# Attention in a hybrid encoder block: score products handed out one bank at a time, the meta keys' transposes moved to the end of their unit, and two reads of PSUM banks put first

## The chip, the cores and the metric

The program runs on one core of a Trainium2 chip. The metric is device microseconds of one execution. The kernel before took 1441.15 us, the median of three runs (1440.94 to 1446.21). A separate profiled execution took 1447.76 us, and its trace is the source of every duration below. Of the engines, TensorE is PE in the profile (its weight loads are PEld), VectorE is DVE, ScalarE is ACT, GpSimd is POOL, and SyncE, which only issues DMAs, is SP.

## The reference, cut to what matters

The block puts 16 meta tokens ahead of 1024 positions of width 1024 (1040 rows in all) and runs a mixer (attention with a forgetting term beside a diagonal state space model with a gated linear unit), an output projection and a gated convolutional feed-forward network. The part that most of the change touches is the attention:

```python
log_f = log_sigmoid(f_logit + b_forget)
cum_f = cumsum(log_f, axis=1)
# per block of 128 queries, 8 heads of width 64:
s = einsum('bqhd,bkhd->bhqk', qb, k) * scale + cum_f[query] - cum_f[key]
s = where(key_position <= query_position, s, -1e30)
p = softmax(s, axis=-1)
out = einsum('bhqk,bkhd->bqhd', p, v)
```

## The kernel before

All matmuls take 32-bit operands that are split into a high and a low part, so that a dense product is three matmuls (`dense_steps`, L172 to L174: high by high, low by high, high by low). TensorE's results go to PSUM banks in four tags: `mm` (three banks, dense products), `sp` (two, scores), `tp` (two, transposes) and `po` (one, the sum over keys). A bank is written again only when whoever reads it has done so.

**Order.** The program is written as one stream per operation, and a scheduling layer orders each engine's instructions. In the attention the order on TensorE is fixed by hand: `pin` (L807) ties each matmul to the one before. `after(a, b)` (L132) only orders two instructions of one program; it moves an instruction behind another one in its queue. Every engine runs its queue in order, so an instruction that waits holds all that stand behind it.

**Attention.** The eight heads come in four pairs. A pair has eight units: four groups of query tiles, here called A (tiles 0, 1, 2; tile 0 is the meta tokens), B (3, 4), C (5, 6) and D (7, 8), each for both heads (`shapes`, `units`). A unit of tiles c and c+1 goes through `pv` (L854):

- `scores` (L813) makes the softmax weights of one tile. Per bank of up to 512 keys it issues two products (L838, L839) into an `sp` bank; VectorE reads the bank with a fused add and running minimum (L844, twice where the diagonal block is in it) into `pt`; ScalarE then takes the exponential (L849), VectorE the reciprocal (L850), and GpSimd scales `pt` (L851). A tile has 1, 2 or 3 banks (tile 8 has three: 352, 352 and 336 keys). `pt` has four buffers, taken in turn (tiles 0 and 1 share one).
- `meta_keys` (L865) transposes the columns of the 16 meta keys of every tile of the unit (L870) into a `tp` bank; ScalarE (L872) and VectorE (L137, `tm`) copy them as high and low part.
- `turn` (L875) transposes one group of two key blocks (L885, up to four transposes) into a `tp` bank, copied out as `th` (L888) and `tl` (L137).
- The products with the values (L911) add four matmuls per group into `po`, and one last product with the meta keys (L914) ends the unit. `po` is then read by L916 and L917.

`fill(part)` (L933) places dense matmuls of the next pair's projection and of the gates between these steps, as many as `UW` gives the unit. The order in a unit before is: `meta_keys`, `turn` of the first group, `fill`, all score products of the next unit's last tile (`ahead`), then per group: `turn` of the next group, `fill`, the products; with the last group, all score products of the first tile (or two) of the unit after next (`behind`). Units A have one group, B two, C three, D four.

**Earlier, around 180 to 200 us.** `forget` (L532) computes the forgetting logits into three `mm` banks; ScalarE (L545) and VectorE (L546) read each, the middle one in two parts (columns 248 and 136). In the same queues stand the casts and splits of the linear unit's operands (`load_z`, L636: casts L648 and L670, low parts L137, one difference on GpSimd at L664). The next dense products on TensorE, the query projection, take the same banks in turn.

**Behind the attention.** When the last L914 has run, the memory of the attention is free, and SP loads `mr`, `ga` and `wr` (L1053, L1052, L1074) there. TensorE works on one gate chunk meanwhile (72 matmuls that are ordered behind the last L911), then on the attention's output product (L1118 to L1120); VectorE reads its banks (L1121), and `out_forms` (L1080) casts (L1097) and splits (L137, `xhi<-wr`) the output weights.

Of the kernel before, what the change touches and what calls it, by code (L numbers as in the profile page):

```python
# [25 lines left out]
H = 8  # L26
# [32 lines left out]
def block_kernel(ctx, tc, x, meta, xbt, x0t, g1t, w_q, w_k, w_v, w_f, w_u, w_g, b_f, w_ao, lam_d, bw_d, cw_d,  # L59
# [347 lines left out]
    for k0, n in FIRST:  # L407
        j, sl = k0 // 2, slice(k0 % 2, k0 % 2 + n)
# [121 lines left out]
    FR = 32 + H  # L530

    def forget():  # L532
# [3 lines left out]
        for t, n in BLK:  # L536
            ps = mm_ps()
            for i in range(KD):
                PE.matmul(ps[:64, :n], wf[:, i, :], xhi[:, i, t:t + n], start=(i == 0), stop=False)
                PE.matmul(ps[:64, :n], wf[:, i, :], xlo[:, i, t:t + n], start=False, stop=(i == KD - 1))  # L540
            for r, a in ((0, 0), (32, HL)):
                lo, up_ = max(t, a), min(t + n, a + HL)
                if lo < up_:
                    sl, ri = slice(lo - a, up_ - a), slice(r, r + H)
                    S.copy(fx[ri, sl], ps[32 - r:32 - r + H, lo - t:up_ - t])  # L545
                    V.scalar_tensor_tensor(out=fl_[ri, sl], in0=ps[ri, lo - t:up_ - t], scalar=bf[ri], in1=fx[ri, sl],  # L546
                                           op0=ALU.add, op1=ALU.add)
# [88 lines left out]
    def load_z():  # L636
# [23 lines left out]
        for k in range(2):  # L660
# [6 lines left out]
            for f_, t_ in zip((fa, fa, fb, fb), (T1, T2, T3, T4)):  # L667
                q = 0 if t_ is T1 or t_ is T3 else TH
                hi, lo = t_[0][:, k], t_[1][:, k]
                after(S.copy(hi, f_[:, q:q + TH]), ssm_outs[6])  # L670
# [142 lines left out]
    def scores(t_, e, c, fb):  # L813
# [21 lines left out]
        for b in range(nb):  # L835
            a0, a1 = b * w, min(kc, b * w + w)
# [15 lines left out]
        return pt  # L852

    def pv(h, cs, pts, ob, ahead, behind):  # L854
# [37 lines left out]
        part = 1 / (1 + len(groups))  # L892
        meta_keys()
        nxt = turn(groups[0])
        if len(groups) > 1:
            fill(part)
            ahead()
        else:
            ahead()
            fill(part)  # L900
        for g_, grp in enumerate(groups):
            th, tl = nxt
            if g_ + 1 < len(groups):
                nxt = turn(groups[g_ + 1])
            else:
                behind()
            fill(part)
# [12 lines left out]
    UW = {2: 1.2, 4: 1.0, 6: 0.95, 8: 0.9}  # L920
# [60 lines left out]

    def scores_of(u, which):
# [9 lines left out]
        pts_of.setdefault(u, [])  # L992
        for c in (cs[:-1] if which == 0 else cs[-1:]):
            pts_of[u].append(scores(tiles_of[pr], e, c, fbs[pr, e]))
# [4 lines left out]
    for u, which, n in ((0, 0, 7), (0, 1, 14), (1, 0, 7)):  # L999
        scores_of(u, which)  # L1000
        take(n)
        cnt -= n
    for u, (pr, cs, e) in enumerate(units):
# [10 lines left out]
        pv(2 * pr + e, cs, pts_of.pop(u), obs[cs], lambda: scores_of(u + 1, 1), lambda: scores_of(u + 2, 0))  # L1014
# [65 lines left out]
    def out_forms(p, j):  # L1080
# [17 lines left out]
        if p in (0, 4):  # L1098
            split_lo(V, slot[3], b_, slot[2])
# [979 lines left out]
```

## Time and profile before

| what | us |
|---|---|
| median of three runs | 1441.15 |
| profiled execution, its own time | 1447.76 |
| span of its trace | 1444.9 |
| TensorE busy | 1416.6 (98%) |
| VectorE busy | 1071.6 (74%) |
| ScalarE busy | 719.8 (50%) |
| GpSimd busy | 760.5 (53%) |

The page counts an engine as busy while an instruction of it runs. Matmuls overlap: the next one starts before the one ahead has ended, so the distance from one start to the next is what a matmul costs TensorE, and the duration in a row is longer than that. An idle time in a row stands in brackets, with whoever ended it. The trace's clock begins at the first instruction.

### The profile page before, as it was taken

Reading aid. Unit: us, or ns where it says so; the run is one execution under the profiler, and the core shown is the slowest. Engines: PE = TensorE matmul, PEld = TensorE weight load, DVE = VectorE, ACT = ScalarE, POOL = GpSimd, SP = SyncE. Lnnn points to the kernel's source line nnn. Section 1 sums busy time; section 2 is a strip of 40 time slices with the busy share of each in tenths; the row PEclk is TensorE's granted clock in tenths of the full one; section 3 lists DMA queues with packets and bytes.
Section 4 is the critical chain, followed back from the end, with each engine's and each line's share of the span. In section 5 each row is a group of like instructions: output and inputs, shape, how many; then the busy total and the mean of one; then the engine's idle time right before and its main releaser. Section 6 shows DMA issues by size and latency. Waiting matters only on the chain.

```text
span 1444.9 us, 26277 instructions
## 1 busy us (share of the span) xinstructions
PE 1416.6 (98%) x9607; PEld 1337.8 (93%) x9607; DVE 1071.6 (74%) x2050; ACT 719.8 (50%) x1405; POOL 760.5 (53%) x866
## 2 busy tenths in 40 slices
PE   8999999999999999999999999999999999999997
PEld 8999989988999999899879999999999999888886
DVE  7999778843667675647469987788777875798867
ACT  7646575423556565532645544444443445553443
POOL 1542248642455555515871244555645446699695
PEclk9999999999999999999999999999999999999999
DMA  8685634530144432157964155677654227863443
GB/s 297 174 183 164 153 96 125 169 118 30 38 154 111 140 81 68 45 190 245 279 151 144 61 150 146 163 183 204 173 142 106 88 93 248 323 224 124 131 95 117
DMA packets 92533, 214.02 MB, mean 148 GB/s; under 512 B 14658, under 2 KB 22466, under 8 KB 92020
## 3 DMA queue, kind: packets, MB, share of 16 engines
q1 hardware_dynamic: 73700, 168.15, 35.0%
q0 software_dynamic: 17696, 41.29, 15.0%
q10 hardware_dynamic: 1008, 2.91, 0.6%
q8 instruction: 75, 1.23, 0.3%
q14 instruction: 54, 0.44, 0.1%
HBM read 170.88 MB, written 71.71 MB: 168 GB/s over the span
## 4 chain that ended last, share of the span: by engine, by line
PE 90%; DMA 3%; POOL 2%; DVE 2%; ACT 1%; issue 1%; SPq 0%; POOLq 0%; DVEq 0%; ACTq 0%
PE mm L173 5%; PE mm L172 5%; PE mm L174 5%; PE sp L235 4%; PE sp L234 4%; PE sp L236 4%; PE mm L236 3%; PE mm L234 3%; PE tp L235 3%; PE tp L234 3%; PE mm L235 3%; PE tp L236 3%; PE po L911 2%; PE mm L1602 2%; PE mm L1600 2%; PE mm L1601 2%
## 5 line engine op out<-in xcount | busy, mean ns | idle before, releaser
L172 PE MATMUL mm<-xhi,whi 128*128 128x342 f32 (+2 forms) x480 | 158.0, 329 | 2.6 <-DVE fg L546 2.6
L173 PE MATMUL mm<-xlo,whi 128*128 128x342 f32 (+2 forms) x480 | 156.7, 326 | 0.0
L174 PE MATMUL mm<-xhi,wlo 128*128 128x342 f32 (+2 forms) x480 | 155.4, 324 | 0.0
L1222 POOL TENSOR_TENSOR ov<-ov,og 128x1024 f32<-128x1024 f32 x21 | 50.8, 2421 | 116.8 <-ACT og L1221 114.4
L137 DVE TENSOR_TENSOR sw<-sf,sw 128x512 fp32r<-128x512 f32 x72 | 71.7, 996 | 46.7 <-ACT sw L1213 46.7
L1213 ACT CAST sw<-sf 128x512 fp32r<-128x512 f32 x72 | 44.9, 624 | 110.2 <-POOL sf L1360 75.7
L172 PEld LDWEIGHTS mm<-xhi,whi 128*128 128x128 f32 x480 | 91.1, 190 | 3.5 <-issue 3.4
L174 PEld LDWEIGHTS mm<-xhi,wlo 128*128 128x128 f32 x480 | 90.9, 189 | 0.3 <-issue 0.2
L173 PEld LDWEIGHTS mm<-xlo,whi 128*128 128x128 f32 x480 | 91.1, 190 | 0.1
L849 ACT ACTIVATE pt<-pt,mx 128x400 f32<-128x400 f32 (+5 forms) x72 | 53.1, 737 | 61.7 <-DVE mx L844 61.0
L1360 POOL TENSOR_TENSOR sf<-raw 128x512 f32<-128x512 f32 x36 | 49.9, 1386 | 64.4 <-DMA raw<-in_w_up_dram 28.8
L1360 POOL TENSOR_TENSOR sf<-raw,sf 128x512 f32<-128x512 f32 x36 | 61.1, 1697 | 38.9 <-DVE sw L137 38.8
L236 PE MATMUL mm<-xhi,sw 128*128 128x258 f32 (+1 forms) x288 | 81.1, 282 | 0.0
L234 PE MATMUL mm<-xhi,sw 128*128 128x258 f32 (+1 forms) x288 | 80.9, 281 | 0.0
L235 PE MATMUL mm<-xlo,sw 128*128 128x258 f32 (+1 forms) x288 | 80.8, 281 | 0.0
L1412 DVE SCALAR_TENSOR_TENSOR ov<-hv,cwt,ov 128x1024 f32<-128x1024 f32 x36 | 70.8, 1967 | 0.4 <-ACT ov L1410 0.4
L851 POOL TENSOR_SCALAR pt<-pt,mx 128x400 f32<-128x400 f32 (+5 forms) x72 | 50.6, 704 | 32.2 <-DVE mx L850 26.6
L1213 ACT CAST sw<-raw 128x512 fp32r<-128x512 f32 x70 | 43.0, 620 | 47.3 <-PE sp L236 24.9
L137 DVE TENSOR_TENSOR tl<-tp,th 128x512 fp32r<-128x512 f32 (+1 forms) x80 | 50.9, 636 | 13.3 <-ACT th L888 12.5
L137 DVE TENSOR_TENSOR sw<-raw,sw 128x512 fp32r<-128x512 f32 x70 | 56.2, 806 | 4.7 <-ACT sw L1213 4.4
L822 POOL CAST qz<-q 64x128 fp32r<-64x128 f32 (+1 forms) x72 | 20.0, 281 | 75.2 <-PE sp L839 74.0
L888 ACT CAST th<-tp 128x512 fp32r<-128x512 f32 (+1 forms) x80 | 43.0, 537 | 29.8 <-PE tp L885 28.3
(724 smaller groups left out, 5732.1 us busy)
## 6 DMA issues: line engine op xcount, KB each, us to landing
raw<-in_w_up_dram SPq DMA_DIRECT2D x44, 512.0 KB, 3.8
t_d<-in_w_dn_dram POOLq DMA_DIRECT2D x44, 256.0 KB, 6.9
wr<-t_d SPq DMA_DIRECT2D x44, 256.0 KB, 3.8
ar<-a_d SPq DMA_DIRECT2D x41, 256.0 KB, 4.9
a_d<-ov SPq DMA_DIRECT2D x18, 512.0 KB, 2.6
wr<-in_w_dn_dram SPq DMA_DIRECT2D x33, 256.0 KB, 3.9
t_d<-in_w_dn_dram SPq DMA_DIRECT2D x22, 256.0 KB, 4.5
t_d<-t_d SPq DMA_DIRECT2D x22, 256.0 KB, 4.9
```

Of the source, the lines that this page charges most:

```text
L137: return eng.tensor_tensor(out_, src, hi.bitcast(F), ALU.subtract)
L172: yield PE.matmul(ps, whi[:, i, :], ahi[:, i], start=(i == 0), stop=False)
L173: yield PE.matmul(ps, whi[:, i, :], alo[:, i], start=False, stop=False)
L174: yield PE.matmul(ps, wlo[:, i, :], ahi[:, i], start=False, stop=(i == k - 1))
L234: PE.matmul(ps, a[0][:, i], bh, start=(i == 0 and not joins), stop=False, skip_group_check=True)
L235: PE.matmul(ps, a[0][:, i], bl, start=False, stop=False, skip_group_check=True)
L236: PE.matmul(ps, a[1][:, i], bh, start=False, stop=(i == kh - 1), skip_group_check=True)
L849: S.activation(pt[:n, :kc], pt[:n, :kc], AF.Exp, bias=low, scale=-1.0, accum_out=nm[:n, 0:1])
L1213: S.copy(hi, src)
L1222: (V if c == NFF - 1 else GP).tensor_tensor(v_, v_, g_, ALU.mult)
L1360: sums.append(GP.tensor_tensor(f_, a, b, op))
L1412: V.scalar_tensor_tensor(out=o, in0=h_[:, j:SEQ + j], scalar=cwc(j, m), in1=o, op0=ALU.mult, op1=ALU.add)
```

## The change

It has five parts, all of them changes of order. No arithmetic instruction is added or removed.

1. `scores` becomes a generator that stops after each bank's products. `pv` gets the pieces of the next unit's last tile and of the unit after next's first tile in one sequence, and hands them out evenly: at each of its spots (one behind each `turn`, and one behind `meta_keys`) it gives out a share of the pieces, each followed by a share of the fill.
2. `meta_keys` stands behind the last group's `turn` and not ahead of the first.
3. `UW`, the weights that share the fill between units, goes from 1.2, 1.0, 0.95, 0.9 to 1.3, 1.0, 0.95, 0.85.
4. The cast of `T3`, first half (L670, `z3h`), is ordered behind the last read of a bank by `forget` (L545).
5. The split of the first output weight (`out_forms`, `p == 0` and `j == 0`) is ordered behind the first sum `added[0]` (L1122).

```diff
@@ forget
-                    S.copy(fx[ri, sl], ps[32 - r:32 - r + H, lo - t:up_ - t])
+                    forget_reads.append(S.copy(fx[ri, sl], ps[32 - r:32 - r + H, lo - t:up_ - t]))
@@ load_z
-                after(S.copy(hi, f_[:, q:q + TH]), ssm_outs[6])
+                cast = S.copy(hi, f_[:, q:q + TH])
+                after(cast, ssm_outs[6])
+                if t_ is T3 and k == 0:
+                    after(cast, forget_reads[-1])
@@ scores
         for b in range(nb):
+            if b:
+                yield
...
-        return pt
+        done.append(pt)
+        yield
@@ pv
-        part = 1 / (1 + len(groups))
-        meta_keys()
+        spots = 1 + len(groups)
+        at = [0]
+
+        def between():
+            at[0] += 1
+            k = -(-count * at[0] // spots) + (-count * (at[0] - 1) // spots)
+            for _ in range(k):
+                next(pieces, None)
+                fill(1 / spots / k)
+            if not k:
+                fill(1 / spots)
+            if at[0] == spots:
+                for _ in pieces:
+                    pass
+
         nxt = turn(groups[0])
-        if len(groups) > 1:
-            fill(part)
-            ahead()
-        else:
-            ahead()
-            fill(part)
+        between()
         for g_, grp in enumerate(groups):
             th, tl = nxt
             if g_ + 1 < len(groups):
                 nxt = turn(groups[g_ + 1])
             else:
-                behind()
-            fill(part)
+                meta_keys()
+            between()
...
-    UW = {2: 1.2, 4: 1.0, 6: 0.95, 8: 0.9}
+    UW = {2: 1.3, 4: 1.0, 6: 0.95, 8: 0.85}
...
-        pv(2 * pr + e, cs, pts_of.pop(u), obs[cs], lambda: scores_of(u + 1, 1), lambda: scores_of(u + 2, 0))
+        pv(2 * pr + e, cs, pts_of.pop(u), obs[cs], chain_(scores_of(u + 1, 1), scores_of(u + 2, 0)),
+           n_pieces(u + 1, 1) + n_pieces(u + 2, 0))
@@ out_forms
         if p in (0, 4):
-            split_lo(V, slot[3], b_, slot[2])
+            cut = split_lo(V, slot[3], b_, slot[2])
+            if p == 0 and j == 0:
+                after(cut, added[0])
```

What this does to the queues is shown at three places. Line numbers of the kernel before are used in the text; in the rows of the changed kernel they stand a few lines higher (L838 is L844 there, L885 is L892, L870 is L877, L911 is L926, L914 is L929, L545 is L546, L670 is L671).

TensorE, second pair, a unit D of the first head, behind its first transposes: `tp<-ident,pt` is a transpose, `sp<-k,q` and `sp<-kl,qz` are the two products of one score bank, here of tile 8 of the second head, and `mm<-` rows are fill. Before:

```order
L172 MATMUL mm<-xhi,whi 128x342
L173 MATMUL mm<-xlo,whi 128x342
L174 MATMUL mm<-xhi,wlo 128x342
L172 MATMUL mm<-xhi,whi 128x342
L838 MATMUL sp<-k_4189,q_4187 128x352
L839 MATMUL sp<-kl,qz_4180 128x352
L838 MATMUL sp<-k_4189,q_4187 128x352
L839 MATMUL sp<-kl,qz_4180 128x352
L838 MATMUL sp<-k_4189,q_4187 128x336
L839 MATMUL sp<-kl,qz_4180 128x336
L885 MATMUL tp<-ident,pt 128x128 x4
```

The changed kernel, from the same transposes on:

```order
L892 MATMUL tp<-ident,pt 128x128 x4
L844 MATMUL sp<-k_4189,q_4187 128x352
L845 MATMUL sp<-kl,qz_4180 128x352
L172 MATMUL mm<-xhi,whi 128x342
L173 MATMUL mm<-xlo,whi 128x342
L174 MATMUL mm<-xhi,wlo 128x342
L172 MATMUL mm<-xhi,whi 128x342
L892 MATMUL tp<-ident,pt 128x128 x4
L844 MATMUL sp<-k_4189,q_4187 128x352
L845 MATMUL sp<-kl,qz_4180 128x352
L173 MATMUL mm<-xlo,whi 128x342
```

The three score banks of tile 8 stood together, behind the first fill. Now the first stands right behind the first transposes, the second behind the second, and the third, not shown, behind the third, with fill and products with the values between them.

ScalarE, at about 185 to 196 us: `fg<-mm` are the reads of the forgetting logits' banks, `mm_2365` is the middle bank, and `z3h` is the cast of part 4, which takes what GpSimd makes at L664. Before:

```order
L545 COPY fg_2344<-mm_2346 8x272
L670 CAST z3h_2436<-zf_2486 128x520
L545 COPY fg_2344<-mm_2365 8x248
L648 CAST zh1_2434<-zt_2463 128x8x130
L684 CAST ops_2729<-raw_2877 128x256
L670 CAST z1h_2440<-zf_2501 128x520
L545 COPY fg_2344<-mm_2365 8x136
L545 COPY fg_2344<-mm_2386 8x384
L602 CAST q0_2517<-po_2529 64x272
```

The changed kernel:

```order
L546 COPY fg_2344<-mm_2346 8x272
L546 COPY fg_2344<-mm_2365 8x248
L649 CAST zh1_2434<-zt_2463 128x8x130
L688 CAST ops_2729<-raw_2877 128x256
L671 CAST z1h_2440<-zf_2501 128x520
L546 COPY fg_2344<-mm_2365 8x136
L546 COPY fg_2344<-mm_2386 8x384
L671 CAST z3h_2436<-zf_2486 128x520
L603 CAST q0_2517<-po_2529 64x272
```

The cast `z3h<-zf_2486` moved behind the four reads; the other rows kept their order. On VectorE the split that belongs to it moved in the same way.

TensorE at the end of the attention: `po<-tl,vt` ends the last group's products, `po<-tm,vt` is the last unit's product with the meta keys, and the `mm<-` rows are the gate chunk that follows. Before:

```order
L911 MATMUL po<-th,vt 128x256
L911 MATMUL po<-tl,vt 128x256
L914 MATMUL po<-tm,vt 128x256
L172 MATMUL mm<-xhi,whi 128x342
L173 MATMUL mm<-xlo,whi 128x342
```

The changed kernel, with the rows left out all of the gate chunk:

```order
L926 MATMUL po<-th,vt 128x256
L926 MATMUL po<-tl,vt 128x256
L172 MATMUL mm<-xhi,whi 128x342
L173 MATMUL mm<-xlo,whi 128x342
L174 MATMUL mm<-xhi,wlo 128x342
...
L173 MATMUL mm<-xlo,whi 128x342
L174 MATMUL mm<-xhi,wlo 128x342
L929 MATMUL po<-tm,vt 128x256
L172 MATMUL mm<-xhi,whi 128x342
L173 MATMUL mm<-xlo,whi 128x342
```

The last product with the meta keys stood right behind the last group's products. Now 18 matmuls of the gate chunk stand between, so 54 of its 72 come behind it and not 72.

On VectorE, behind the attention, the split of the first output weight moved behind the first sum. The split of the second weight, which shared a row with it, now stands behind the first and ahead of the second of the bank reads at L1121.

19 lines of the change are left out of this document (13 added, 6 removed).

## Prediction

> **What bounds the kernel now.** I first read the busy time by stage (columns: length, then busy time of PE, PEld, DVE, ACT and POOL, the granted clock, the DMA share). The second stretch is the attention.
>
> ```profile
> 200.00:349.00 149.00, 148.58 (x1006) 138.54 (x1005) 97.56 (x181) 66.06 (x153) 73.52 (x99) 1.00 0.36 113
> 349.00:626.00 277.00, 267.74 (x1860) 257.38 (x1859) 177.90 (x622) 156.15 (x367) 145.55 (x281) 1.00 0.29 83
> ```
>
> TensorE is the bound in both: in the attention it is idle for 9.3 of 277 us, and the next engine, VectorE, is busy for 178. So a change of order can give back only TensorE's own waits. The second view is TensorE's waits (us in total, times, longest):
>
> ```profile
> PE sp L838 <- DVE mx L844: 6.5, 11, 1.5
> ...
> PE mm L172 <- DVE fg L546: 2.6, 1, 2.6
> PE tp L870 <- POOL pt L851: 1.7, 4, 0.9
> PE mm L1118 <- DVE ga L1121: 1.2, 1, 1.2
> ...
> PE tp L885 <- DVE tm L137: 0.8, 2, 0.4
> ```
>
> The first is a score product that waits for one of the two `sp` banks, the third a transpose that waits for softmax weights, the last a transpose that waits for a `tp` bank: 9.0 us in the attention. The other two are the waits that parts 4 and 5 aim at. The third view is the timeline around each.
>
> **Part 4, the read of the forgetting logits' bank.**
>
> ```profile
> 195.00 0.34 PE L174 MATMUL mm<-xhi,wlo 128*128 128x384 f32 x1
> 197.98 0.66 PE L172 MATMUL mm<-xhi,whi 128*128 128x384 f32 x1 [2.65 <-DVE fg L546]
> ...
> 201.00 0.36 PE L172 MATMUL mm<-xhi,whi 128*128 128x384 f32 x1
> 201.19 0.34 PE L173 MATMUL mm<-xlo,whi 128*128 128x384 f32 x1
> ...
> 198.00:200.00 2.00, 2.00 (x6) 2.00 (x7) 1.94 (x3) 1.09 (x2) 0.63 (x1) 0.50 0.20 41
> ```
>
> Undisturbed starts lie 0.19 apart. From 195.00 to 197.98 it is 2.98, so the wait costs 2.8. Then the granted clock is 0.50 and the nine matmuls up to 201.00 take 3.02 where 9 x 0.19 = 1.7 is due: 1.3 more. The wait is worth 4.1 us. [...]
>
> Does the read come in time after the change? The queues of the two readers before:
>
> ```profile
> 187.14 0.38 ACT L545 COPY fg<-mm 8x272 f32<-8x272 f32 x1
> 190.86 0.63 ACT L670 CAST z3h<-zf 128x520 fp32r<-128x520 f32 x1 [3.34 <-POOL zf L664]
> 191.39 0.35 ACT L545 COPY fg<-mm 8x248 f32<-8x248 f32 x1
> 191.65 2.34 ACT L648 CAST zh<-zt 128x1040 fp32r<-128x1040 f32 x1
> ...
> 194.02 2.49 DVE L137 TENSOR_TENSOR zl<-zt,zh 128x1040 fp32r<-128x1040 f32 x1 [1.43 <-ACT zh L648]
> 196.44 0.41 DVE L137 TENSOR_TENSOR ops<-raw,ops 128x256 fp32r<-128x256 f32 x1
> 196.77 0.68 DVE L137 TENSOR_TENSOR z1l<-zf,z1h 128x520 fp32r<-128x520 f32 x1
> 197.48 0.88 DVE L546 SCALAR_TENSOR_TENSOR fg<-mm,bf,fg 8x136 f32<-8x136 f32 x2
> ...
> 185.47 5.35 POOL L664 TENSOR_TENSOR zf<-zt 128x520 f32<-128x520 f32 x1
> 196.79 1.84 POOL L664 TENSOR_TENSOR zf<-zt 128x520 f32<-128x520 f32 x1 [2.28 <-DVE zl L137]
> ```
>
> ScalarE stood idle for 3.34 behind GpSimd's difference. Without `z3h` in front, the 248-column read starts at 187.5, `zh` runs to 187.5 + 0.35 + 2.34 = 190.2, and VectorE, whose order otherwise stays, does `zl`, `ops`, `z1l` and the 136-column read: 190.2 + 2.49 + 0.41 + 0.68 + 0.44 = 194.2. TensorE wants the bank at 195.2: 1.0 us of cover. `z3h` itself now comes at about 192 and holds up only the query casts behind it, which stood at 195.4. What is late next are the linear unit's operands; VectorE starts them about 3 us earlier while TensorE comes 4.1 earlier, and the stretch from 200 has TensorE at 148.58 of 149. I take **-4.1** (between 0 and -4.1).
>
> **Parts 1 to 3, the attention.** A bank wait and a switch in full:
>
> ```profile
> 474.39 0.32 PE L838 MATMUL sp<-k,q 128*128 128x352 f32 x1
> 474.55 0.32 PE L839 MATMUL sp<-kl,qz 128*128 128x352 f32 x1
> 476.33 0.42 PE L838 MATMUL sp<-k,q 128*128 128x336 f32 x1 [1.46 <-DVE mx L844]
> ...
> 454.39 0.60 PE L885 MATMUL tp<-ident,pt 128*128 128x128 f32 x4
> 454.75 0.42 PE L172 MATMUL mm<-xhi,whi 128*128 128x384 f32 x1
> 455.01 0.34 PE L173 MATMUL mm<-xlo,whi 128*128 128x384 f32 x1
> 455.18 0.34 PE L174 MATMUL mm<-xhi,wlo 128*128 128x384 f32 x1
> ```
>
> From 474.55 to 476.33 it is 1.78 where 0.16 is due, so the wait costs 1.62, 0.16 more than the bracket says. Over the 17 waits of the attention that makes 9.0 + 17 x 0.16 = 11.7 us.
>
> *Removed.* The third bank of a tile was asked for 0.3 us after the first; now at least 0.7 us of fill, and mostly a group of transposes too, lie between two pieces, and VectorE needs some 0.5 for a bank. The bank waits should go, and so should the `tp` waits, since the meta keys no longer take a bank just ahead of two groups. I count all **-11.7** as removed and book below what comes back.
>
> *Added: switches.* The first matmul behind transposes takes 0.26 (454.75 to 455.01), the next 0.17: each change from transposes to products costs 0.085 us. `meta_keys` stood next to the first `turn` and shared its change; alone it adds one to each of the 32 units: **+2.7**.
>
> *Added: waits for weights.* The last bank of a tile must be followed in time by its softmax. That chain before:
>
> ```profile
> 478.14 1.17 ACT L849 ACTIVATE pt<-pt,mx 128x1040 f32<-128x1040 f32 x1
> ...
> 479.69 1.13 POOL L851 TENSOR_SCALAR pt<-pt,mx 128x1040 f32<-128x1040 f32 x1 [1.16 <-DVE mx L850]
> ```
>
> From the product at 476.33 to 479.69 + 1.13 = 480.82 it is 4.5 us. In the first three pairs the last bank of tile 8 lies three spots ahead of the unit's end, about 5 us ahead of its use. In the last pair it moves to the fourth spot of five, and what follows it is 9 fills x 0.16, 8 products at 0.12 (estimated from the matmuls' columns), the meta keys' transposes and two changes: 3.1 to 3.3 us, so about 1.3 us of wait. Of the 1.7 + 4 x 0.16 = 2.3 us at L870, all but one behind GpSimd's four weight splits, I leave half, since those splits stand ahead of the same scaling in the new queue: 1.1.
>
> *Added: waits for the meta keys.* `tm` used to be ready a whole unit ahead of L914; now a fill and four products lie between. Moreover the meta keys' transposes are now the last readers of the unit's `pt`, and `pt` has four buffers, so VectorE's first pass over the tile of the unit after next must wait for them, and `tm` stands behind that pass. In units D:
>
> ```profile
> 414.21 0.16 DVE L844 CUSTOM_DVE_ANT_0 pt<-sp,fm 16x16 f32<-16x16 f32 x1 [0.33 <-PE sp L839]
> ...
> 415.00 0.15 DVE L850 RECIPROCAL mx<-mx 16x1 f32<-16x1 f32 x1
> ...
> 416.64 0.41 DVE L137 TENSOR_TENSOR tm<-tp,tm 16x256 fp32r<-16x256 f32 x1
> ```
>
> The two small tiles take 0.8 and `tm` 0.41; with 0.35 for the transpose to land (an estimate, from the 0.33 that VectorE waited for a product) and 0.2 for the second tile's product, `tm` is there 1.8 us behind the transposes, and L914 is due at 1.6: about 0.2 in six units, **1.2**. Units A to C have more fill there and need none. New waits together: 1.3 + 1.1 + 1.2 = **+3.6** (from 0 to the 11.7 that went). `UW` moves fill by one or two matmuls per unit and stays at nothing.
>
> The attention: -11.7 + 2.7 + 3.6 = **-5.4**.
>
> **Part 5 and the 18 matmuls.**
>
> ```profile
> 625.17 0.28 PE L914 MATMUL po<-tm,vt 128*128 128x256 f32 x1
> ...
> SPq L1053 <- PE po L914: 19.9, 1, 19.9
> ...
> 643.04 1.14 ACT L1097 CAST xhi<-wr 128x512 fp32r<-128x512 f32 x2 [5.41 <-DMA wr<-in_w_o_dram]
> 643.70 1.29 DVE L137 TENSOR_TENSOR xhi<-wr,xhi 128x512 fp32r<-128x512 f32 x2 [5.70 <-ACT xhi L1097]
> 644.91 1.35 DVE L1121 TENSOR_TENSOR ga<-mm,ga 128x342 f32<-128x342 f32 x3
> ...
> 645.47 0.42 PE L1118 MATMUL mm<-k,whi 128*128 128x342 f32 x1 [1.15 <-DVE ga L1121]
> ```
>
> The chain is L914, SP's loads, `wr` landed at 643.04 (17.9 behind L914), two casts, two splits, the read of the bank, TensorE: 1.15, and 0.16 that the bracket leaves out, make 1.3 us lost. Part 5 takes the first split out of the way of the first read, which alone would remove this. But the second split still stands ahead of the second read, and SP's loads, SP's queue being held at L914, now start 18 x 0.16 = 2.9 us later against TensorE's own work. Counted from L914, the second split is done when the reads begin, at 644.91 - 625.17 = 19.7, and the second read, a third of 1.35, at 20.1; its bank is due 12 products (12 x 0.16 = 1.9) behind the first, at 645.47 - 1.3 + 1.9 - 2.9 - 625.17 = 18.0. So 2.1 us are lost, not 1.3: **+0.8** (from -1.3 to +2).
>
> **Sum.** -4.1 - 5.4 + 0.8 = -8.7. The profiled execution took 1447.76, of which 1444.9 is span; the rest does not change, so it would take 1439.1. The runs' median lies 6.6 lower, at 1441.15, and I carry the difference over: **1432.5 us**, -0.6%.
>
> **Rivals.**
>
> *The waits change place.* TensorE no longer waits for banks, but as long for weights and for `tm`: the new waits are 11.7 and not 3.6. For it: VectorE and ScalarE work in order, and three kinds of work share them. Against it: they are busy for 178 and 156 of 277 us. -4.1 + 2.7 + 0.8 = -0.6: 1440.5.
>
> *The bank is read late all the same.* GpSimd's difference took 5.35 us beside a busy VectorE and 1.84 the second time. If VectorE now works through without a pause and is itself the one held up, by those 3.5 us, the read ends at 197.7 and TensorE stands as before. [...] Part 4 is then worth nothing: 1436.6.
>
> *Slower: exponentials ahead of `tm`.* If in units B, C and D ScalarE's queue has an exponential that waits for VectorE's held pass between the transposes and the cast of `tm`, L914 is late by up to 1.17 - 0.3 = 0.9 us in each of 24 units: 21, less the 1.2 booked, so 1432.5 + 20 = 1452. It ends above the old time from 0.41 us a unit on ((8.7 + 1.2) / 24). Against it: only in the last pair's unit D does such an exponential stand there.
>
> *All clean.* No new wait, and the loads land in time: -4.1 - 11.7 + 2.7 - 1.3 = -14.4: 1426.8.
>
> **Chances.** Forecast 0.50, waits change place 0.18, late bank 0.12, all clean 0.14, slower 0.06. Half a per cent, 7.2 us, is about what a measurement of this kernel can tell from no change, so faster means below 1433.9. The forecast's own terms spread by some 4 us, which leaves about 0.7 of its 0.50 below that: 0.35 + 0.14 gives 0.49, taken as 0.50; slower 0.06; the rest, 0.44, is the same. The range goes from the clean case to the moved waits, 1426.5 to 1440.5.
>
> **What would show it.** Right: in TensorE's waits of the changed kernel L838 is gone from the list or below 1 us, L172 behind `fg` is gone and the granted clock stays 1.00 around 198, and L1118 shows about 2 us in one or two waits. Waits at L914 behind `tm` should come to about 1 us in units D, and one of about a microsecond should stand at the last pair's last unit. Wrong: waits of L885 or L914 of more than 5 us in all, `zl` on VectorE ending behind 194, or score products still waiting at L838.

## The result, and the profile after

The changed kernel took 1438.35 us (median of 20 runs, 1436.17 to 1443.47), the kernel before 1444.78 beside it (20 runs, 1440.65 to 1449.05). The ratio is 0.996, with a 95% interval of 0.9949 to 0.9971: 4.2 to 7.4 us, about 5.8, faster (the two medians lie 6.4 apart). By the half per cent of the prediction that is no change that counts. The profiled execution took 1440.54 us with a span of 1438.7, so 7.2 and 6.2 us less than the one before. Lines are those of the changed kernel.

TensorE's waits (us in total, times, longest):

```profile
PE po L929 <- DVE tm L137: 3.8, 6, 1.4
...
PE mm L172 <- DVE fg L547: 0.8, 1, 0.8
PE tp L892 <- POOL pt L857: 0.7, 2, 0.4
PE po L926 <- DVE tl L137: 0.5, 2, 0.3
...
PE po L926 <- DVE ob L932: 0.5, 2, 0.3
PE sp L844 <- DVE mx L850: 0.4, 1, 0.4
```

The score products wait once, at the start of the attention, where they did before; the wait at the output product is gone. In their place the last product of a unit waits for `tm`, and products with the values (L926), which never waited before, wait for VectorE.

To see where the time went I cut the timeline at TensorE's instructions that both kernels have: the last forgetting product, the first product of the linear unit, the first score product, the last gate product, the last product of the attention's output. Of the kernel before, then of the changed one:

```profile
187.77 0.34 PE L540 MATMUL mm<-xlo,wf 128*64 128x384 f32 x1
...
215.15 0.28 PE L234 MATMUL mm<-zh,ops 128*128 128x260 f32 x1
...
347.54 0.17 PE L838 MATMUL sp<-k,q 128*32 128x16 f32 x1
...
636.45 0.32 PE L174 MATMUL po<-xhi,wlo 128*128 128x342 f32 x1
...
683.28 0.32 PE L1120 MATMUL po<-ohi,wlo 128*128 128x342 f32 x1
```

```profile
188.76 0.34 PE L541 MATMUL mm<-xlo,wf 128*64 128x384 f32 x1
...
212.93 0.28 PE L234 MATMUL mm<-zh,ops 128*128 128x260 f32 x1
...
345.71 0.17 PE L844 MATMUL sp<-k,q 128*32 128x16 f32 x1
...
631.25 0.31 PE L174 MATMUL po<-xhi,wlo 128*128 128x342 f32 x1
...
676.99 0.32 PE L1146 MATMUL po<-ohi,wlo 128*128 128x342 f32 x1
```

- From the last forgetting product to the first product of the linear unit: 27.38 before, 24.17 after, -3.2 (where part 4 lies; kernel 4 below shows that it is not its doing).
- The attention with its last gate chunk: 288.9 before, 285.5 after, -3.4 (parts 1 to 3).
- The output stretch, up to the last output product: 46.8 before, 45.7 after, -1.1.

Together -7.7. The rest adds up to +1.4, 1.0 of it ahead of the forgetting products, where nothing was changed, and makes it the span's -6.2.

### The profile page after: what moved, and what is told of

It is laid out like the page before. It is cut to its first block, busy times and chain, and to the rows that moved or that the text cites. A ratio compares the mean times of both kernels' runs of the same rounds, so it can differ in the third digit from the quotient of the medians.

```text
span 1438.7 us, 26301 instructions
## 1 busy us (share of the span) xinstructions
PE 1415.4 (98%) x9607; PEld 1337.6 (93%) x9607; DVE 1076.2 (75%) x2050; ACT 720.9 (50%) x1405; POOL 759.4 (53%) x866
## 4 chain that ended last, share of the span: by engine, by line
PE 56%; DMA 1%; DVE 0%; issue 0%; ACT 0%; POOLq 0%; DVEq 0%; POOL 0%
PE sp L235 4%; PE sp L234 4%; PE sp L236 4%; PE tp L235 2%; PE tp L234 2%; PE tp L236 2%; PE mm L236 2%; PE mm L234 2%; PE mm L235 2%; PE mm L1628 2%; PE mm L1626 2%; PE mm L1627 2%; PE mm L1293 2%; PE mm L1294 2%; PE mm L1292 2%; PE sp L1628 1%
## 5 line engine op out<-in xcount | busy, mean ns | idle before, releaser
L172 PE MATMUL mm<-xhi,whi 128*128 128x342 f32 (+2 forms) x480 | 155.1, 323 | 0.8 <-DVE fg L547 0.8
L895 ACT CAST th<-tp 128x512 fp32r<-128x512 f32 (+1 forms) x80 | 42.9, 544 | 33.5 <-PE tp L892 27.4
```

The source lines that it names most:

```text
L172: yield PE.matmul(ps, whi[:, i, :], ahi[:, i], start=(i == 0), stop=False)
```

## The experiments

Each kernel was timed beside the kernel before and profiled once. The table has the ratio of times with its interval, and from the profiled execution the three stretches named above and the waits in the attention, by who waits. A wait is counted here as the distance from one start to the next less the usual distance (in ns, 7 and 0.4375 a column for a product, 109 for a transpose: estimates from the profile before, where 23 distances at 384 columns took 4.05 us, 24 at 272 columns 3.01, and four transposes last 0.60 and one 0.273), where more than 0.15 us is over. The 0.6 us that the very first score product waits in every kernel is left out, and sums are of unrounded numbers.

| kernel | ratio | forgetting | attention | its waits: score banks, transposes, values, tm = sum | output |
|---|---|---|---|---|---|
| before | 1 | 27.4 | 288.9 | 8.2, 4.2, 0, 0 = 12.4 | 46.8 |
| changed | 0.9960 (0.9949 to 0.9971) | 24.2 | 285.5 | 0, 1.0, 2.7, 5.0 = 8.7 | 45.7 |
| 1: changed, meta keys first | 1.0043 (1.0028 to 1.0059) | 23.1 | 295.0 | 0.2, 18.4, 0, 0 = 18.6 | 46.2 |
| 2: before, meta keys last | 0.9961 (0.9948 to 0.9974) | 23.1 | 285.2 | 5.4, 2.5, 0.2, 0 = 8.1 | 45.4 |
| 3: before, more changes of kind | 1.0033 (1.0021 to 1.0044) | 23.2 | 293.5 | 9.7, 3.5, 3.7, 0 = 16.8 | 45.5 |
| 4: before, parts 4 and 5 | 1.000 (0.9989 to 1.001) | 23.1 | 289.6 | 8.9, 4.3, 0, 0 = 13.2 | 46.8 |
| 5: as 2, last unit's meta keys first | 0.9971 (0.996 to 0.9982) | 23.1 | 285.7 | 5.2, 2.7, 0.5, 0 = 8.3 | 46.1 |
| 6: changed, old fill weights | 0.9953 (0.9938 to 0.9968) | 23.1 | 281.9 | 0, 2.6, 0.2, 2.2 = 4.9 | 45.4 |
| 7: changed without part 5 | 0.996 (0.9944 to 0.9976) | 23.1 | 285.2 | 0, 1.0, 2.7, 4.7 = 8.3 | 45.4 |
| 8: parts 1 and 2 alone | 0.9953 (0.9936 to 0.997) | 23.1 | 281.7 | 0, 2.6, 0.2, 2.1 = 4.9 | 45.5 |
| 9: next unit's pieces spread alone | 0.9959 (0.9945 to 0.9974) | 23.1 | 284.2 | 0.3, 5.6, 0.8, 0.9 = 7.5 | 45.4 |
| 10: other fill weights | 0.9955 (0.9939 to 0.9971) | 23.1 | 284.5 | 0.2, 3.5, 1.9, 2.3 = 7.9 | 45.4 |
| 11: as 2, new fill weights | 0.9984 (0.9972 to 0.9996) | 23.1 | 288.2 | 6.9, 0.3, 3.2, 0.9 = 11.4 | 45.7 |

The times tell kernels apart only where they differ by some 3 us; the stretches do so more finely. The attention of the changed kernel and of kernel 7, whose attention has the same order, differ by 0.4 us, that of kernels 6 and 8 by 0.2, that of the kernel before and of kernel 4 by 0.7; each comes from one execution.

### 1. The meta keys first

My first theory put the new waits down to the meta keys' place at the end.

```diff
+        meta_keys()
         nxt = turn(groups[0])
         between()
...
             if g_ + 1 < len(groups):
                 nxt = turn(groups[g_ + 1])
-            else:
-                meta_keys()
             between()
```

> The changed kernel, with the meta keys' transposes put back ahead of the first group's transposes; the score pieces stay spread. Theory 1 (the meta keys' place): in the attention of the changed kernel 8.7 us of waits are new, 5.0 of them at the product with tm and 1.0 at transposes, and they come from handing the meta keys out last. Then the wait at the product with tm falls from 3.8 us in six times to nearly nothing, the score products still wait for nothing, 1 to 3 us of waits for pt and for a tp bank come back, and the kernel is 2 to 5 us faster than the changed one (some 9 to 11 us, 0.6 to 0.8%, faster than before). Theory 2 (VectorE's queue): the spread pieces crowd VectorE and ScalarE whatever the place of the meta keys; the waits change place and stay at 8 to 9 us, and the time stays within 1.5 us of the changed kernel's.

It became 0.43% slower than before. Its waits on TensorE, and one of them, with VectorE's and ScalarE's rows beside it:

```profile
PE tp L892 <- DVE tm L137: 12.3, 10, 2.0
...
PE tp L877 <- POOL pt L857: 3.3, 6, 1.5
```

```profile
458.34 0.60 PE L892 MATMUL tp<-ident,pt 128*128 128x128 f32 x4
...
462.56 0.63 PE L892 MATMUL tp<-ident,pt 128*128 128x128 f32 x4 [2.04 <-DVE tm L137]
...
459.40 1.12 DVE L137 TENSOR_TENSOR kl<-mm,k 64x384 fp32r<-64x384 f32 x2 [1.77 <-ACT k L613]
...
461.40 0.57 DVE L850 CUSTOM_DVE_ANT_0 pt<-sp,fb,mx 128x352 f32<-128x352 f32 x1
...
462.00 0.41 DVE L137 TENSOR_TENSOR tm<-tp,tm 16x256 fp32r<-16x256 f32 x1
```

The meta keys and the first group take both `tp` banks. The second group's transposes need the meta keys' bank, and `tm`, which reads it, stands on VectorE behind a split of 1.12 us and behind reads of score banks. In the kernel before, with the bunched scores, all three score banks lay between the first and the second group. Spread, the groups are closer together, and the price is 18.4 us of waits at transposes for 4.2. (The 0.2 at score banks in the table is no wait that the profile lists: there the very first score product alone waits, 0.42 us by its bracket.) Theory 1 is refuted: with spread pieces, part 2 is needed. Theory 2 had the waits at 8 to 9 us and the time as in the changed kernel, and misses both.

### 2. The meta keys last, and nothing else

```diff
-        meta_keys()
         nxt = turn(groups[0])
...
             else:
+                meta_keys()
                 behind()
```

> The kernel before with one step of the change: the meta keys' transposes go last in their unit, the score products stay bunched. Theory 1 (the meta keys' place): waits at the product with tm appear here too, 3 us or more, beside bank waits of about 8 us as before, less the 3.0 at the meta keys' transposes: 0 to 3 us slower than before. Theory 2 (VectorE's queue): the product with tm waits only where pieces are spread, so less than 1 us here, and the time is 1 to 3 us below the one before.

There is no wait at `tm`, so theory 1 falls. Theory 2 had that right, but neither theory had a third of the bank waits gone with the scores still bunched; why they went stays open. This one step gives as much as the whole change, 0.9961, with 3.7 us off the attention and 1.4 off the output stretch.

```profile
PE sp L838 <- DVE mx L844: 4.2, 9, 1.2
...
PE tp L885 <- POOL pt L851: 1.5, 5, 0.7
```

Compared with the rows of before (6.5 in 11 times, 1.7 in 4), the bank waits are most of what fell (8.2 to 5.4 in the table), and L885 no longer waits for `tm`.

### 3. The price of a change from transposes to products

```diff
                     pin(PE.transpose(tp[:, o:o + P], p_[:, k0:k0 + P], ident))
+                if gi == 0:
+                    take(1)
```

> The kernel before, with one fill product taken into the middle of each group of transposes that has both key blocks (about 80 groups), so that each has one change from transposes to products more; nothing else. By the prediction's price of 0.085 us a change this costs 6 to 7 us. By the trace of the changed kernel, where the product behind the last transpose of a group starts 0.03 us behind it and not 0.11, and the next one 0.08 late, the two cancel: under 0.5 us, within what the waits around it scatter.

The kernel is 4.8 us slower (0.33% of 1443.9 us), which looks like the prediction's price. It isn't: the attention took 4.6 us longer, and its waits 4.4 (16.8 for 12.4, mostly at the values, 3.7, and at score banks, 1.5 more). Attention less waits is 276.5 before with 80 changes, 276.8 in the changed kernel with 112, and 276.7 here with 152. So 72 more changes cost about 0.2 us, 3 ns each, and the 32 of the changed kernel 0.3. The same remainder lies between 276.4 and 277.4 over all kernels of the table, so these are sizes within the scatter; 0.085 us a change would have been 6.1.

### 4. Parts 4 and 5 alone

The edits are those of the change, on the kernel before.

> The kernel before with parts 4 and 5 alone, which lie 450 us apart and can be read one by one in the trace. Part 4: as in the changed kernel, the wait at the forgetting logits' bank falls from 2.6 to about 0.8 us and the clock stays full: 3.3 us off; by the prediction it is gone and 4.1 come off; by the rival with a late read nothing comes off. Part 5: SP's queue keeps its old order here. If the order of the split alone did it, the 1.3 us at the output product go here too. If SP's earlier loads of the changed kernel (wr 14.7 us behind the last product with the meta keys, 17.9 before) were needed, a wait of 0.5 us or more stays. Both together: 4 to 5 us, 0.3%, faster than before.

The time did not move (1.000, 0.9989 to 1.001). For part 4 the table has the reason: the forgetting stretch takes 23.1 us here, and as much in kernels 2, 3, 5, 8 and 11, which do not have part 4. The 27.4 of the profile before was not what that kernel usually takes. The same place in kernel 2, whose code there is that of before:

```profile
184.88 1.59 POOL L664 TENSOR_TENSOR zf<-zt 128x520 f32<-128x520 f32 x1
...
185.19 1.83 DVE L137 TENSOR_TENSOR z2l<-zf,z2h 128x520 fp32r<-128x520 f32 x1
...
193.34 0.88 DVE L546 SCALAR_TENSOR_TENSOR fg<-mm,bf,fg 8x136 f32<-8x136 f32 x2
```

GpSimd's difference took 1.59 where it took 5.35 in the profile before, the 136-column read started at 193.34 and not at 197.48, and TensorE did not wait for it. For part 5 a wait of 1.1 us is left, with VectorE's rows behind it:

```profile
639.89 0.69 DVE L137 TENSOR_TENSOR xhi<-wr,xhi 128x512 fp32r<-128x512 f32 x1 [6.11 <-ACT xhi L1101]
640.50 1.35 DVE L1127 TENSOR_TENSOR ga<-mm,ga 128x342 f32<-128x342 f32 x3
...
641.06 0.43 PE L1124 MATMUL mm<-k,whi 128*128 128x342 f32 x1 [1.09 <-DVE ga L1127]
```

The first split has moved, but one split still stands ahead of all three reads.

### 5. The last unit's meta keys first

Against kernel 2:

```diff
+        end = h == H - 1 and main[-1] is pts[-1] and cs[-1] == 8
+        if end:
+            meta_keys()
         nxt = turn(groups[0])
...
-                meta_keys()
+                if not end:
+                    meta_keys()
```

> The kernel before with the meta keys' transposes last, but ahead of the first group in the very last unit. There the last product with the meta keys stands right behind the products with the values again, and on SyncE the store of a gate chunk and a weight load stand behind the three loads into freed memory again. Theory 5 (SyncE's order): the 1.1 to 1.4 us that the output product gained in the changed kernel and in the run with the meta keys last come from this order alone, part 5 aside. Then wr lands 17 to 18 us behind the last product with the meta keys and not 13.5 to 14.7, the stretch from the last gate product to the last output product is 46.7 us and not 45.4, and a wait of about 1.2 us behind the read of the bank is back. Rival: the gain comes from TensorE being earlier in the attention; then the stretch stays at 45.4 to 45.8.

SyncE's queue in the kernel before, and in the changed kernel:

```profile
625.49 1.28 SPq L1053 DMA_DIRECT2D mr<-m_d  x3
627.05 0.41 SPq L514 DMA_DIRECT2D g_d<-gs  x1
...
630.52 0.39 SPq L1074 DMA_DIRECT2D wr<-in_w_o_dram  x1
```

```profile
621.91 0.33 SPq L514 DMA_DIRECT2D g_d<-gs  x1
623.13 1.56 SPq L1077 DMA_DIRECT2D mr<-m_d  x3
...
625.99 0.69 SPq L1098 DMA_DIRECT2D wr<-in_w_o_dram  x1
```

Before, the store `g_d<-gs` stood behind the loads into freed memory (`mr<-m_d`); now it goes out while those still wait, and `wr` is issued 3.2 us behind the last product with the meta keys (622.83) in place of 5.4. Kernel 5 has the old queue: `wr` was used 17.2 us behind that product (634.73 - 617.58), a wait of 0.5 is back, and the stretch takes 46.1.

```profile
617.58 0.28 PE L918 MATMUL po<-tm,vt 128*128 128x256 f32 x1
...
634.73 1.14 ACT L1101 CAST xhi<-wr 128x512 fp32r<-128x512 f32 x2 [4.75 <-DMA wr<-in_w_o_dram]
...
637.15 0.42 PE L1122 MATMUL mm<-k,whi 128*128 128x342 f32 x1 [0.49 <-DVE ga L1125]
```

The load came as late as theory 5 had it, but the stretch is 0.7 us longer than in kernel 2 and not 1.3. Nor is that 0.7 shown to come from SyncE's order, because VectorE's order differs as well. In the kernel before, both splits stand ahead of all three reads of the banks (the prediction shows the rows, 643.70 and 644.91), and so they do in kernel 5. In kernel 2 the first read stands between the two splits, and in the changed kernel ahead of both (638.70 is the second weight's split, the first's comes later):

```profile
637.46 0.50 DVE L1147 TENSOR_TENSOR ga<-mm,ga 128x342 f32<-128x342 f32 x1
638.70 0.69 DVE L137 TENSOR_TENSOR xhi<-wr,xhi 128x512 fp32r<-128x512 f32 x1 [0.73 <-ACT xhi L1121]
639.31 0.93 DVE L1147 TENSOR_TENSOR ga<-mm,ga 128x342 f32<-128x342 f32 x2
```

Against TensorE's work the load is hardly earlier in the changed kernel: `wr` is used 6.3 us behind the last gate product (637.53 - 631.25), in the kernel before 6.6. With both splits ahead of the first read, TensorE would have waited about 1 us there too. That is an estimate from the rows of the kernel before: 0.7 us from the use of `wr` to the first split, 1.2 for both splits and 0.6 from the read to the product that waited put this product 8.8 us behind the last gate product, and in kernels 2 and 7, without a wait, it stands at 7.7. The order on VectorE keeps the changed kernel from that. An early load can do it alone as well: kernel 3, whose fill lies otherwise, has VectorE's old order and the early store (SyncE issues it at 624.03, the loads from 625.41), uses `wr` 3.7 us behind the last gate product, and takes 45.5 us without any part of the change. How the 1.4 us divide between the two orders is open.

### 6. The old fill weights

```diff
-    UW = {2: 1.3, 4: 1.0, 6: 0.95, 8: 0.85}
+    UW = {2: 1.2, 4: 1.0, 6: 0.95, 8: 0.9}
```

> The changed kernel with the old fill weights (part 3 undone). Theory 6 (part 3 costs nothing): waits in the attention 8.7 us as in the changed kernel, within 1 us, and the same time within 1.5 us. Rival: the smaller share of the units D is why the product with tm waits at their ends; then the waits in units D at tm fall by 1 us or more.

Theory 6 falls and the rival holds: undoing part 3 takes 3.7 us off the attention. The waits at the values fall from 2.7 to 0.2, those at `tm` from 5.0 to 2.2 (in units D from 4.0 to 2.2), and transposes wait 1.6 more.

```profile
PE tp L892 <- POOL pt L857: 1.8, 5, 0.7
PE po L929 <- DVE tm L137: 1.4, 3, 0.7
```

What such a wait is made of, in the changed kernel, at a product with the values:

```profile
453.19 1.12 DVE L137 TENSOR_TENSOR kl<-mm,k 64x384 fp32r<-64x384 f32 x2 [0.74 <-ACT k L613]
454.35 0.42 DVE L932 TENSOR_TENSOR ob<-po,ob 64x256 f32<-64x256 f32 x1
454.80 0.69 DVE L137 TENSOR_TENSOR tl<-tp,th 128x512 fp32r<-128x512 f32 x1
...
454.91 0.36 PE L926 MATMUL po<-th,vt 128*128 128x256 f32 x1 [0.26 <-DVE ob L932]
455.54 0.39 PE L926 MATMUL po<-tl,vt 128*128 128x256 f32 x1 [0.27 <-DVE tl L137]
```

and at the longest wait for `tm`:

```profile
546.70 0.39 PE L929 MATMUL po<-tm,vt 128*128 128x256 f32 x1 [1.42 <-DVE tm L137]
...
544.88 1.06 ACT L994 CAST k<-kl 128x1040 fp32r<-128x1040 f32 x1 [0.86 <-DMA kl<-o_d]
545.84 0.36 ACT L879 CAST tm<-tp 16x256 fp32r<-16x256 f32 x1
```

In both, what is in the way is no score: a split of the next pair's keys (1.12 us), and a cast that waited 0.86 for a load and then took 1.06. I take it that how the fill is shared out decides beside which products such work falls; the runs show only that other weights move the waits.

### 7. Without part 5

```diff
-            cut = split_lo(V, slot[3], b_, slot[2])
-            if p == 0 and j == 0:
-                after(cut, added[0])
+            split_lo(V, slot[3], b_, slot[2])
```

> The changed kernel with part 5 undone; everything else, SyncE's order too, is as there. Theory 5 (SyncE's order): with wr in 3 us earlier, the two splits are done before TensorE wants the bank, as in the run with the meta keys last, which has no part 5 and no wait there: the stretch from the last gate product to the last output product stays at 45.4 to 45.8 us. Rival (the order of the split): a wait of 0.6 us or more behind the read of the bank is back, and the stretch is 46.3 us or longer.

45.4 us with no wait: the rival falls, and part 5 does nothing here either. The stretch is what theory 5 said, but the first read stands between the two splits here (as in kernel 2), so this run does not show that SyncE's order alone does it.

### 8. Parts 1 and 2 alone

The edits are those of kernels 6 and 7, and part 4 is taken out:

```diff
-                if t_ is T3 and k == 0:
-                    after(cast, forget_reads[-1])
```

> The changed kernel with parts 3, 4 and 5 undone: only the spread pieces and the place of the meta keys are left. Theory 7 (these two are all of it): the attention takes 282 us as with the old fill weights, the stretch from the last gate product to the last output product 45.4, the stretch from the last forgetting product to the linear unit 23.1 as in the other runs without part 4, and the time is that of the run with the old fill weights (0.9953 of before) within 1.5 us. Rival: part 4 takes off what the profile of the kernel before showed, 4.1 us, in the usual execution too; then this kernel is 3 to 4 us slower than the one with the old fill weights.

Stretches and ratio are those of kernel 6: theory 7 holds, and the rival falls. Spreading the pieces and moving the meta keys are all of the gain, the 1.3 us of the output stretch among it, and kernels 6 and 8 have the lowest ratios, 0.9953. Against the changed kernel the two intervals overlap; that they beat it rests on the attention, 3.7 and 3.9 us shorter in one execution each. Their profiled executions are the shortest of their timed runs, that of the changed kernel lies 2.2 us above its median; against kernel 7, which was profiled near its median, they are 3.3 and 3.5 shorter.

### 9. Only the next unit's pieces spread

```diff
-        at = [0]
+        at, left = [0], [count]
...
-            k = -(-count * at[0] // spots) + (-count * (at[0] - 1) // spots)
-            for _ in range(k):
-                next(pieces, None)
-                fill(1 / spots / k)
-            if not k:
-                fill(1 / spots)
+            k = 1 if at[0] < spots - 1 else count if at[0] == spots - 1 else 0
+            for _ in range(min(k, left[0])):
+                next(pieces)
+                left[0] -= 1
             if at[0] == spots:
                 for _ in pieces:
                     pass
+            fill(1 / spots)
```

`count` is that of the next unit's last tile alone, and the old fill weights stand.

> The changed kernel, with the meta keys' transposes last as there, but only the score pieces of the next unit's last tile spread, one to a spot ahead of the last spot; those of the unit after next stand together behind the meta keys' transposes, as the kernel before had them, and the fill weights are the old ones. The run with the meta keys last and all pieces bunched had no wait at the product with tm, 5.4 us of waits for score banks and 2.5 us at transposes; the changed kernel had none for banks, but 5.0 us at the product with tm and 2.7 at the products with the values. Theory 3 (cover of the last spot): the waits at tm and at the values come from spreading the pieces out of the last spots, where they covered the copies; the bank waits left come from the three banks of tile 8 together. Then both go here: 3 to 4 us of waits in the attention in place of 8.7 and 8.1, and 4 to 5 us less time than the changed kernel, 0.7% less than before. Theory 4 (a full queue): VectorE's and ScalarE's queues hold the same work and the waits only change place again: 7 us or more, and no more than 1.5 us below the changed kernel.

The eight timed executions of that first run took 1434.77 to 1439.5 us (ratio 0.9957, 0.9941 to 0.9972). The profiled one says nothing about waits, so the kernel was run again:

> The same kernel as in the run with only the next unit's pieces spread, whose profiled execution ran at about a fifth of the usual speed and shows no waits that can be read. Theory 3 (cover of the last spot): 3 to 4 us of waits in the attention, below the 4.9 of the changed kernel with the old fill weights, none at the product with tm, and a time 1 to 2 us below that kernel's 0.9953 of before. Theory 4 (a full queue): 5 us of waits or more, at other places, and the same time as that kernel.

The waits at `tm` nearly go, as theory 3 had it, but 5.6 us come back at transposes that wait for weights, and the sum of 7.5 is above the 4.9 of kernel 6. Theory 4 holds: the waits are at other places, and the time is the same within the noise.

### 10 and 11. Other fill weights

```diff
-    UW = {2: 1.3, 4: 1.0, 6: 0.95, 8: 0.85}
+    UW = {2: 1.2, 4: 1.0, 6: 1.0, 8: 0.85}
```

> The changed kernel with the fill weights 1.2, 1.0, 1.0, 0.85: units A as before the change, which leaves 117 fill products ahead of units C as before and not 121, and units D with 23 in place of 24 (22 and 23 in the changed kernel), the rest in units C. Theory 8 (where the projection's splits fall): in the changed kernel the products with the values of units C wait 2.7 us because four more fill products in units A and B bring VectorE's two splits of the next pair's keys (1.12 us) right ahead of the low parts of the first transposes of units C; with 117 ahead that wait is gone (under 0.5 us), while the wait at tm stays near 2.2 to 5.0. Rival (units D have too little fill): the waits at the values stay, or all the extra waits are at tm in units D and stay as in the changed kernel, 5.0 us.

Theory 8 falls: the waits at the values are 1.9 and not under 0.5. With 117 fill products ahead of units C, 1.5 of the 1.9 are still in units C, at the second head's and no longer at the first's. Kernel 11 is kernel 2 with the new weights (1.3, 1.0, 0.95, 0.85), so part 3 with bunched pieces:

> The kernel before with the meta keys last (bunched pieces) and the new fill weights: parts 2 and 3 without part 1. Theory 9 (part 3 costs by the place at which it puts the fill, with bunched pieces too): the waits in the attention, 8.1 us with the old weights, come to 10 us or more, and the attention to 287 us or more. Rival (part 3 costs only where pieces are spread): 7.5 to 8.7 us of waits and 285.4 us of attention, as with the old weights.

Theory 9 holds: 11.4 us of waits for 8.1, the attention 3.0 longer. So, with the meta keys last, the two steps stand apart: spreading the pieces takes 3.4 us off the attention with the old weights (285.2 to 281.8, the mean of kernels 6 and 8) and 2.8 with the new (288.2 to 285.4, the mean of the changed kernel and kernel 7); the new weights cost 3.6 with spread pieces and 3.0 without. The times show it less well: 3.3 us between kernels 11 and 2, whose intervals just touch, and 1.0 between the changed kernel and kernel 6, which is within the noise. What a table of weights costs was not seen ahead in any of the three tried; why just 1.2 and 0.9 do well stays open.

## Why the prediction was right or wrong

It said -8.7 us; about 5.8 were measured, and the traces account for 4.5 of them (attention -3.4, output stretch -1.1); the rest lies within the interval. The time fell in the range, and the size was too large (1432.5 was counted from 1441.15, and the kernel before took 1444.78 beside the changed one). That it was not further off is luck: part 4 and the new waits promised 9.2 us too much, and the other terms 5.0 too little.

- **Part 4, -4.1: wrong, it is worth nothing.** The step that failed is the price: one execution's wait was taken as the kernel's. The wait itself was read well, that execution lost 4.2 us by it (27.4 less 23.1; starts lie 0.175 apart there, and not the 0.19 that was read right behind the slow clock). The step right behind it made that worse: the 6.6 us between the profiled execution and the median of three runs were carried over whole, though the wait was most of them, so it was taken off a median that did not have it. Five traced executions without part 4 show no such wait, and part 4 with part 5 moved no time. The rival of a late read came nearer: in the changed kernel's own profile VectorE's operations were the long ones (`ops` 1.23 us for 0.41), and TensorE waited 0.8 us with part 4 in place (the last section).
- **Bank and other waits removed, -11.7: right.** It was 12.4, and score products wait for nothing any more (but for the very first, as before). That spreading alone does it was not right: with the pieces still bunched, part 2 took 8.2 us of bank waits to 5.4.
- **Changes from transposes to products, +2.7: wrong.** It is about 0.3. I read the second product behind the transposes, 0.085 late, and not the first. The rows were quoted: four transposes from 454.39, the first product at 454.75, 0.36 later, where four transposes of 0.11 make 0.44. What the second loses, the first has gained.
- **New waits, +3.6: too small, 8.7, and the largest miss.** `UW` "stays at nothing" is the step that failed: 3.8 of the 5.1 that are missing are its, and without it the new waits are 4.9 (kernel 6). The parts were off too: with `UW`, 5.0 at `tm` where 1.2 was said, 1.0 at weights for 2.4, and 2.7 at the values, which I had not looked at. The estimate for `tm` counted score reads ahead of it, and the long ones stand behind splits and casts of the projection and of other work in the same queues. The sum for the last pair has a slip besides: the terms that it lists (9 x 0.16, 8 x 0.12, two transposes of 0.11, two changes of 0.085) make 2.8 and not 3.1 to 3.3.
- **Part 5 and the 18 matmuls, +0.8: wrong sign, -1.1.** The step that failed is the load's delay: the text had SyncE's loads 2.9 us later against TensorE's work, and `wr` was used 0.3 us earlier (6.3 behind the last gate product for 6.6). That the 18 products ahead of the last L914 also let a store and a load on SyncE go out ahead of them, I had not followed up, nor that the first read of a bank comes ahead of a split without part 5 too (kernels 2 and 7). Part 5 itself is worth nothing that these runs can show.
- **The rivals.** "The waits change place" was the nearest: 8.7 came for 12.4. The slower one needs an exponential ahead of `tm`; in the longest wait it was another cast of the same length, in one unit of 32 and not in 24.
- **The signs.** L838 nearly gone and the clock at 1.00 came as said for right. The wait behind `fg` stayed at 0.8 us, none came at the output product where 2 us were said, and the waits at L885 and L914 come to 6.0 us by the table (4.5 by the profile's brackets), where more than 5 was to mean wrong.
- **The chances.** 0.50 for faster by over half a per cent hung on part 4; without its 4.1 the same sum reads -4.6, and "no change" would have been the likeliest.

## What to carry to other kernels

A wait that one profiled execution shows is priced by several executions, or by how far that execution lies from the median, before it goes into a sum. Where the bounding engine is full, moving work gains only if what comes late next is counted for all that stands in the same queues, splits and casts of other stages among it; a table that shares out fill is such a move. And when an instruction that frees memory or a buffer moves, read each DMA queue for what is now ahead of it.

## What the runs showed of the hardware

Two things had not been expected. GpSimd's difference of 520 columns and VectorE's split `z2l` run side by side, and which of them is long differs from one execution to the next. In the profile before GpSimd took 5.35 us, while `z2l` took 0.68; in the profiles of the changed kernel and of kernels 1 to 4 GpSimd took 1.57 to 1.59 us and `z2l` 1.82 to 1.83. In the changed kernel `ops`, an operation of VectorE beside GpSimd's next difference, took longer too:

```profile
187.29 1.57 POOL L665 TENSOR_TENSOR zf<-zt 128x520 f32<-128x520 f32 x1
...
187.59 1.82 DVE L137 TENSOR_TENSOR z2l<-zf,z2h 128x520 fp32r<-128x520 f32 x1
...
194.23 1.23 DVE L137 TENSOR_TENSOR ops<-raw,ops 128x256 fp32r<-128x256 f32 x1
194.41 0.75 POOL L694 TENSOR_TENSOR sf<-raw 128x256 f32<-128x256 f32 x1
...
196.64 0.88 DVE L547 SCALAR_TENSOR_TENSOR fg<-mm,bf,fg 8x136 f32<-8x136 f32 x2
...
197.14 0.41 PE L172 MATMUL mm<-xhi,whi 128*128 128x384 f32 x1 [0.81 <-DVE fg L547]
```

`z2l` took 1.82 for 0.68, and `ops` 1.23 for the 0.41 of the profile before, with a difference on GpSimd beside both; the 0.8 us for which TensorE then waits behind `fg` are no more than the 0.8 that `ops` alone lost. What makes them long, and what decides which of the two it is, was not tried.

The second is the hand-over from transposes to products: in the profile before the first product starts 0.03 us behind the last of four transposes (at 454.75, three distances of 0.109 behind 454.39 being 454.72), where transposes lie 0.11 apart, and the next product 0.08 late (0.26 behind the first, for 0.175), so the two nearly cancel. As to the clock, behind the 0.8 us of the changed kernel's wait the granted clock was 1.00, and behind the 2.65 us in the profile before 0.50, from 197.7 to 201.0. In kernel 1 the starts behind TensorE's idle 2.04 us ahead of 462.56 lie as they do without a wait: the first two products behind the transposes are 0.24 apart (462.95 and 463.19), as they were at 458.70 and 458.94. What decides it was not tried. The changed kernel behind its wait:

```profile
198.00:200.00 2.00, 2.00 (x13) 2.00 (x12) 1.89 (x3) 1.72 (x1) 1.56 (x1) 1.00 0.05 12
```
